# A decoder block in fp32: gate sums in raw tiles, the second norm by token tile, the SH1 sums ahead of the first weight tile, a convolution tap on ScalarE, small vectors on GpSimd's queue

## The chip, the cores and the metric

The kernel runs on one core of a Trainium2 chip. TensorE (PE) multiplies matrices, PEld is its loading of the stationary operand, VectorE (DVE) and ScalarE (ACT) do elementwise work, GpSimd (POOL) little, and SyncE (SP) issues the DMAs of the weights. The metric is the device time of one execution in microseconds (us).

## The reference

One block with 256 tokens of 2048 features, everything in fp32; each weight is used once.

```python
mod = silu(c) @ w_ada + b_ada                     # c: one vector of 2048
sh1, sc1, g1, sh2, sc2, g2 = split(mod, 6)
h = rms_norm(x, norm1_g) * (1 + sc1) + sh1
q, k, v, gb, gc, xt = split(h @ w_in, 6)          # 6 x 1024 columns
q, k = rms_norm per head (8 heads of 128)
attn = causal softmax attention(q, k, v)          # 256 tokens are one block
conv = gb * causal_dwconv(gc * xt, conv_w, conv_b)      # 3 taps
mixed = concat(rms_norm(attn), rms_norm(conv))
x = x + g1 * (mixed @ w_out)
h2 = rms_norm(x, norm2_g) * (1 + sc2) + sh2
u = causal_dwconv(h2 @ w_ffn_up, ffn_conv_w, ffn_conv_b)  # 11264 columns
ug, uu = split(u, 2)
x = x + g2 * ((silu(ug) * uu) @ w_ffn_down)
```

## The kernel before

Every weight is split in two on the chip: ScalarE rounds a tile to `hi` (`split_hi`, L246) and VectorE subtracts to get `lo` (`split_lo`, L252). Activations have such halves too, and each product is three matmuls: hi by hi, hi of the weight by lo of the activation, and lo by hi (`mm_tok`, L412 to L415).

The work is a list of slots, one weight tile of about 1 MB each: 48 for `w_in` (the table `turns` sets their order; g, c, v, x, q, k name the six parts, two banks of PSUM for each half), 16 for `w_out`, and then the up and down projections of the FFN in four segments. For slots of `w_in`, the sum of one part stays in its PSUM banks from one slot to the next if the two lie at most `near` slots apart; otherwise it is copied out by ScalarE (L424) or added by VectorE (L426) to `pa_*`. Weights arrive in a ring of raw tiles (`raw`); whoever consumes one calls `load_next`, which puts the next load on SyncE's queue. A tile is split two slots ahead (`LA`).

Beside the weights, 96 MB of `w_ada` have to be multiplied by one vector. These sums (`Ada`, SC1 and SH1 for the first norm, G1 and G2 the gates, SC2 and SH2 for the second norm) lie between the slots, tile by tile, either on TensorE (L297) or on VectorE (L303); the table `ada` says which, and from which slot on. The result is turned into columns (`cols`, L341 to L358: `adac`, `adaz`, `A`, `B`) or, for a gate, spread over the partitions (`spread`, L369).

All other work (convolution, attention, norms, evacuations) is a task with a slot number and a class from the table `cls`, which decides its place in the slot's order. Each engine works through its own list in the order in which the program issues it.

The start: x is loaded and squared, then two tiles of SC1, the first weight tile and two tiles of SH1 are loaded in that order (L1123: `steps[:2] + [("w", 0)] + steps[2:] + [("w", 1)]`). The sums of SC1 and SH1 run on TensorE between the transposes of x (`xn`), and the first `h_chunks` turns them into the first activations `h`, on ScalarE (L862, L864).

The second norm stands between `w_out` and the up-projection: the last product `m('C', 3)`, its evacuation `z` with the gate and the addition to `x1` (`evac_c`, L501, L506), the squares, the root (`n2m`, `n2q`), a diagonal matrix of the reciprocal norms (`n2d`, L604), a product of ones with it that spreads the norm over all partitions (`n2b`, L606), a copy of that (`rB`, L610) and the first `h2` (L629 to L634). TensorE has four tiles of an `ada` sum to do meanwhile. In the up-projection, a product has hi and lo of the activation side by side as 512 columns (L795), which VectorE adds up after (L688), or, where `direct` says so, each by itself with 256 columns into the same half of a bank, with no addition:

```python
for w, v in ((hi, 0), (hi, 1), (lo, 0)):
    mm(o, w[:, j, a], h2T[k + j][:, v * 256:v * 256 + 256], ...)
```

## Time and profile before

| what | value |
|---|---|
| median of 3 runs | 1180.21 us (1179.96 to 1181.82) |
| the profiled execution | 1182.36 us |
| its span | 1180.5 us |
| TensorE busy | 1153.6 us, 98% |
| VectorE busy | 934.8 us, 79% |
| ScalarE busy | 620.3 us, 53% |
| DMA queue of the weights | 314.83 MB, 74.4% of 16 engines |

The span is the time from the first to the last instruction; the 1.9 us around it belong to the execution's own time. An engine's busy time is a sum over stages, which the stretches of the span tell apart. Idle time stands in brackets ahead of the instruction that followed it, with the instruction that released it.

### The profile page before, as it was taken

How to read it: one execution, taken by the hardware profiler on the slowest of the kernel's cores; microseconds unless marked ns; L12 is line 12 of the kernel's file. 1: busy time of each engine (PE TensorE's matmuls, PEld its weight loads, DVE VectorE, ACT ScalarE, POOL GpSimd, SP SyncE). 2: the span in 40 equal slices, each digit the busy share in tenths (PEclk: the TensorE clock that was granted, in tenths of full speed). 3: DMA queues.
4: the chain of work that ended last, by engine and by line, in shares of the span. 5: the costliest groups of instructions: out<-in, count | busy, mean ns of one | idle time of the engine just before them, and what ended most of it. 6: DMA issues, size and time to landing. Idle time of an engine off the chain costs nothing.

```text
span 1180.5 us, 15371 instructions
## 1 busy us (share of the span) xinstructions
PE 1153.6 (98%) x5971; PEld 964.6 (82%) x5971; DVE 934.8 (79%) x1060; ACT 620.3 (53%) x890; POOL 1.2 (0%) x8
## 2 busy tenths in 40 slices
PE   5999999999999999999999999999999999999998
PEld 3777788878877878888888888888888888888887
DVE  3588999999999989989988766887655676576876
ACT  5645265468584555476665434555444455335442
POOL 0000000000000000000000000000000000000000
PEclk9999999999999999999999999999999999999999
DMA  9999999998878789964567988655565556766352
GB/s 364 382 348 389 384 344 376 414 366 319 319 280 308 285 297 330 384 237 155 178 222 259 372 324 319 234 195 179 194 230 172 189 179 208 234 210 203 135 169 89
DMA packets 189181, 317.98 MB, mean 269 GB/s; under 512 B 6922, under 2 KB 106028, under 8 KB 184756
## 3 DMA queue, kind: packets, MB, share of 16 engines
q1 hardware_dynamic: 187780, 314.83, 74.4%
q10 hardware_dynamic: 1328, 2.16, 0.5%
q8 instruction: 47, 0.77, 0.3%
q14 instruction: 26, 0.21, 0.0%
HBM read 312.77 MB, written 4.19 MB: 268 GB/s over the span
## 4 chain that ended last, share of the span: by engine, by line
PE 81%; DVE 10%; DMA 4%; ACT 2%; issue 1%; SPq 0%; ACTq 0%; DVEq 0%
PE z L795 23%; PE z L798 12%; DVE lo L252 4%; DVE ada L303 3%; DMA raw<-in_w_in_dram 2%; PE ada L297 1%; PE mg L414 1%; PE mg L415 1%; PE mg L412 1%; PE mx L414 1%; DMA raw<-in_w_ffn_up_dram 1%; PE mx L415 1%; PE mx L412 1%; DMA raw<-in_w_ada_dram 1%; PE mc L414 1%
## 5 line engine op out<-in xcount | busy, mean ns | idle before, releaser
L252 DVE TENSOR_TENSOR lo<-raw,hi 128x2048 fp32r<-128x2048 f32 (+2 forms) x204 | 448.2, 2204 | 141.5 <-ACT hi L246 125.4
L246 ACT ACTIVATE hi<-raw 128x2048 fp32r<-128x2048 f32 (+2 forms) x204 | 376.1, 1850 | 299.5 <-DMA raw<-in_w_in_dram 80.0
L795 PE MATMUL z<-h,hi 128*128 128x512 f32 x1408 | 329.7, 390 | 2.6 <-DVE h L634 2.0
L795 PEld LDWEIGHTS z<-h,hi 128*128 128x128 f32 x1408 | 261.1, 188 | 56.2 <-DVE h L634 1.4
L303 DVE SCALAR_TENSOR_TENSOR ada<-raw,csil,ada 128x512 f32<-128x512 f32 (+2 forms) x150 | 183.8, 1229 | 3.3 <-DMA raw<-in_w_ada_dram 0.2
L798 PEld LDWEIGHTS z<-h,lo 128*128 128x128 f32 x1408 | 174.8, 192 | 3.4
L798 PE MATMUL z<-h,lo 128*128 128x256 f32 x1408 | 176.0, 283 | 0.0
L688 DVE TENSOR_TENSOR ub<-z,ub 128x256 f32<-128x256 f32 x112 | 39.6, 417 | 34.4 <-ACT ub L685 34.3
L685 ACT ACTIVATE ub<-z 128x256 f32<-128x256 f32 x112 | 33.4, 383 | 35.3 <-PE z L795 35.3
L720 ACT ACTIVATE gh<-uy 128x512 fp32r<-128x512 f32 x22 | 13.9, 632 | 66.8 <-DVE uy L718 66.8
L702 ACT ACTIVATE uy<-ub,fc,fc 128x256 f32<-128x256 f32 x88 | 45.6, 600 | 1.9 <-DVE ub L693 1.9
L709 DVE SCALAR_TENSOR_TENSOR uy<-ub,fc,uy 128x254 f32<-128x254 f32 x88 | 42.5, 484 | 3.1
L707 DVE SCALAR_TENSOR_TENSOR uy<-ub,fc,uy 128x255 f32<-128x255 f32 x88 | 42.1, 479 | 0.1
L297 PE MATMUL ada<-raw,crep 128*32 128x256 f32 (+1 forms) x224 | 23.1, 530 | 7.6 <-DMA raw<-in_w_ada_dram 7.6
L714 ACT ACTIVATE uy<-uy 128x512 f32<-128x512 f32 x22 | 13.8, 627 | 29.7 <-DVE uy L709 29.7
L721 DVE TENSOR_TENSOR gl<-uy,gh 128x512 fp32r<-128x512 f32 x22 | 15.2, 693 | 15.4 <-ACT gh L720 15.4
L414 PE MATMUL mc<-hi,h 128*128 128x512 f32 x64 | 25.6, 400 | 1.1 <-ACT pa_x L424 1.1
L414 PE MATMUL mv<-hi,h 128*128 128x512 f32 x64 | 25.4, 397 | 0.7 <-ACT h L864 0.7
L414 PE MATMUL mg<-hi,h 128*128 128x512 f32 x64 | 25.7, 401 | 0.0
L414 PE MATMUL mx<-hi,h 128*128 128x512 f32 x64 | 25.4, 397 | 0.0
L414 PE MATMUL mk<-hi,h 128*128 128x512 f32 x64 | 25.3, 396 | 0.0
L415 PE MATMUL mq<-hi,hl 128*128 128x512 f32 x64 | 25.0, 391 | 0.2 <-DVE hl L869 0.2
(560 smaller groups left out, 1792.7 us busy)
## 6 DMA issues: line engine op xcount, KB each, us to landing
raw<-in_w_ada_dram SPq DMA_DIRECT2D x96, 1024.0 KB
raw<-in_w_ffn_up_dram SPq DMA_DIRECT2D x176, 512.0 KB
raw<-in_w_in_dram SPq DMA_DIRECT2D x48, 1024.0 KB
raw<-in_w_ffn_down_dram SPq DMA_DIRECT2D x24, 1024.0 KB
raw<-in_w_ffn_down_dram SPq DMA_DIRECT2D x24, 768.0 KB
raw<-in_w_out_dram SPq DMA_DIRECT2D x16, 1024.0 KB
xr<-in_x_dram SPq DMA_DIRECT2D x2, 1024.0 KB
x<-in_x_dram SPq DMA_DIRECT2D x8, 256.0 KB
```

Source lines behind the costliest of these rows:

```text
L246: act(hi[:, :nk], t[:, :nk], AF.Copy)
L252: V.tensor_tensor(out=lo[:, :nk], in0=t[:, :nk], in1=hi[:, :nk].bitcast(F32), op=ALU.subtract)
L297: mm(self.acc[q:q + 32, :], crep[:, i, :], t[:, j, :], start=(r == 0 and j < 4), stop=(r == self.tiles - 1 and j >= self.rows - 4), tile_p ...
L303: V.scalar_tensor_tensor(out=self.acc, in0=t[:, j, :], scalar=csil[:, i:i + 1], in1=self.acc, op0=ALU.mult, op1=ALU.add)
L414: mm(o, a, hi[:, k, s], start=(first and k == 0), stop=False)
L415: mm(o, b, hi[:, k, s], start=False, stop=False)
L688: V.tensor_tensor(out=d, in0=zp[grp][ft][:, :256], in1=d, op=ALU.add)
L702: act(y, b, AF.Identity, bias=fcols[3][:, i:i + 1], scale=fcols[2][:, i:i + 1])
L707: V.scalar_tensor_tensor(out=y[:, 1:], in0=b[:, :255], scalar=fcols[1][:, i:i + 1], in1=y[:, 1:], op0=ALU.mult, op1=ALU.add)
L709: V.scalar_tensor_tensor(out=y[:, 2:], in0=b[:, :254], scalar=fcols[0][:, i:i + 1], in1=y[:, 2:], op0=ALU.mult, op1=ALU.add)
L795: mm(zp[grp][ft], hi[:, j, ft * P:(ft + 1) * P], h2T[k + j], start=begins and j == 0, stop=ends and j == 3)
L798: mm(zp[grp][ft][:, :256], lo[:, j, ft * P:(ft + 1) * P], h2T[k + j][:, :256], start=False, stop=False)
```

## The change

The tables get new values throughout: another order of the slots of `w_in` (it begins with g and c), other slots for the tasks, `near` from 1 to 3, six raw tiles for five, fewer 2 KB buffers. Beyond that:

- `consume` begins with all four tiles of SC1 and SH1, then the first two weight tiles; the first of these is loaded in two halves. TensorE's list at the start has 30 products of constants (`idle`, `spin`). The first slot (`go_first`) takes all hi products ahead of the lo products; its `h` is made by VectorE.
- Of the second quarter of SC1 (L297 before), the sum is on VectorE.
- The sums of G1 and G2 lie in a raw tile (`home`) that is filled with zeros and the bias by GpSimd, which drops the eight loads and additions of the bias.
- The eleven small vectors (`load_v`) are loaded from GpSimd's queue, six slots earlier.
- In the short convolution, the middle tap is multiplied on ScalarE and added by VectorE for two tiles at once (`conv3`, `taps`). Two heads of the attention share a tile when they are split. The sums of squares over attention and convolution (`ss_cols`) go to TensorE one slot later than the last square.
- `evac_c` works by token tile, and the second token tile in two halves of a bank each; each token tile has its own root and its own `n2d`; the first two chunks of `h2` read `n2b` in PSUM, and `rB` is copied behind them.
- `direct` from [0, 0] to [1, 0]: 12 slots of the up-projection.

```diff
- 'bufs': [42, 6, 5, 3, 3],
+ 'bufs': [38, 6, 6, 3, 5],
+ 'spin': [22, 4, 0, 0, 4, 0],
+ 'taps': [1, 0, 0],
- 'near': 1,
+ 'near': 3,
- 'direct': [0, 0],
+ 'direct': [1, 0],
...
+        def home(self):
+            what = f"ada{self.part}_{self.c0}"
+            self.acc = sb.tile([P, 4, 512], F32, tag="raw", bufs=N_RAW, name=what).rearrange("p a b -> p (a b)")
+
+            nc.gpsimd.memset(self.acc, 0.0)
+            a = self.part * D + self.c0 * P
+            nc.gpsimd.dma_start(self.acc[0:1, :], b_ada[0:1, a:a + self.n])
...
+        one(0, slice(0, 512), 0)
+        one(1, slice(0, 256), 1)
+        root(0, 0)
+        one(1, slice(256, 512), 2)
+        nrm["p"] = bank("n2b")
+        diag(0)
+        root(1, 2)
+        diag(1)
...
-        mm(p[:, :256], ones, d, start=True, stop=True)
+        for t in range(2):
+            mm(p[:, t * P:(t + 1) * P], ones, nrm["d", t], start=True, stop=True)
...
+        ks = list(range(cut[0]))
+        h2_chunks(ks[:2], p[:, :256])
         act(rB[0], p[:, :256], AF.Copy)
-        h2_chunks(range(cut[0]), p[:, :256])
+        h2_chunks(ks[2:], rB[0])
...
+                z = t2k("tap")
+                for j in range(2):
+                    s = slice(j * 256, j * 256 + 256)
+                    act(z[:, s], b[:, s], AF.Copy, scale=w[2 - d][:, i + j:i + j + 1])
+                V.tensor_tensor(out=pair(y)[:, :, d:], in0=pair(z)[:, :, :256 - d], in1=pair(y)[:, :, d:], op=ALU.add)
...
-    consume += steps[:2] + [("w", 0)] + steps[2:] + [("w", 1)]
+    consume += steps + [("w", 0), ("w", 1)]
...
+    def spin(i):
+        for _ in range(CFG["spin"][i]):
+            mm(idle[:, :P], ones, ident, start=True, stop=True)
+
     ccol = to_cols(vc, 16, "ccol")
+    spin(0)
...
-                  (q_norm_g, 1), (k_norm_g, 1)], nc.sync)
+                  (q_norm_g, 1), (k_norm_g, 1)], nc.gpsimd)
```

TensorE's list at the start, before (`ada_0_138` is SC1, `ada_0_199` is SH1, `xn` the transposes of x):

```order
L188 MATMUL pv_ccol<-ident,vcb 128x16
L297 MATMUL ada_0_138<-raw,crep 32x256 x16
L188 MATMUL pv_vbc<-ident,vcb 128x112
L1167 MATMUL xn_163<-ident,xr 128x128 x4
L341 MATMUL adac_0_173<-ident,adae_0_170 128x128 x2
L1167 MATMUL xn_185<-ident,xr 128x128 x4
L1167 MATMUL xn_192<-ident,xr 128x128 x4
L297 MATMUL ada_0_199<-raw,crep 32x256 x8
L1167 MATMUL xn_210<-ident,xr 128x128 x4
L1167 MATMUL xn_217<-ident,xr 128x128 x4
L1167 MATMUL xn_224<-ident,xr 128x128 x4
L297 MATMUL ada_0_199<-raw,crep 32x256 x8
```

And now (`ada_0_164` is SC1, `ada_0_228` SH1, `idle` the products of constants):

```order
L194 MATMUL pv_ccol<-ident,vcb 128x16
L1204 MATMUL idle<-ident,ones 128x128 x22
L314 MATMUL ada_0_164<-raw,crep 32x256 x8
L1204 MATMUL idle<-ident,ones 128x128 x4
L314 MATMUL ada_0_164<-raw,crep 32x256 x8
L194 MATMUL pv_vbc<-ident,vcb 128x112
L1234 MATMUL xn_195<-ident,xr 128x128 x4
L349 MATMUL adac_0_203<-ident,adae_0_189 128x128 x2
L1234 MATMUL xn_209<-ident,xr 128x128 x4
L1234 MATMUL xn_214<-ident,xr 128x128 x4
L1234 MATMUL xn_219<-ident,xr 128x128 x4
L314 MATMUL ada_0_228<-raw,crep 32x256 x8
```

Ahead of the two tiles of SC1 now stand 22 and 4 products that use no data from memory; three groups of transposes for two precede SH1.

VectorE's list at the second norm, before, from the last evacuation on:

```order
L501 SCALAR_TENSOR_TENSOR z30_3661<-m('C', 3)0_3585,rC_3213,ada2_0_1535 128x512
L506 TENSOR_TENSOR x1_03_2573<-z30_3661,x1_03_2573 128x512
L501 SCALAR_TENSOR_TENSOR z31_3666<-m('C', 3)1_3586,rC_3213,ada2_0_1535 128x512
L506 TENSOR_TENSOR x1_13_2581<-z31_3666,x1_13_2581 128x512
L599 SCALAR_TENSOR_TENSOR n2m_3671<-n2q_3660,ss2_94 128x2
L200 RECIPROCAL n2r_3672<-n2q_3660 128x2
L201 SCALAR_TENSOR_TENSOR n2q_3660<-n2r_3672 128x2
L202 TENSOR_TENSOR n2q_3660<-n2q_3660,n2m_3671 128x2
L203 SCALAR_TENSOR_TENSOR n2r_3672<-n2q_3660,n2r_3672 128x2
L604 TENSOR_SCALAR n2d_3692<-ident_70,n2r_3672 128x128 x2
L629 SCALAR_TENSOR_TENSOR h2f_3699<-x1T00_3504,A2_92,n2b_3695 128x256
L629 SCALAR_TENSOR_TENSOR h2f_3703<-x1T00_3504,A2_92,n2b_3695 128x256
```

And now:

```order
L610 SCALAR_TENSOR_TENSOR z30_3668<-m('C', 3)0_3542,rC_3204,ada2_0_1428 128x512
L616 TENSOR_TENSOR x1_03_2954<-z30_3668,x1_03_2954 128x512
L610 SCALAR_TENSOR_TENSOR z31_3669<-m('C', 3)1_3543,rC_3204,ada2_0_1428 128x256
L616 TENSOR_TENSOR x1_13_2962<-z31_3669,x1_13_2962 128x256
L620 SCALAR_TENSOR_TENSOR n2m_3665<-n2q_3664,ss2_94 128x1
L610 SCALAR_TENSOR_TENSOR z31_3669<-m('C', 3)2_3544,rC_3204,ada2_0_1428 128x256
L614 SCALAR_TENSOR_TENSOR ss2_94<-n2q_3664,ss2_94 128x1
L616 TENSOR_TENSOR x1_13_2962<-z31_3669,x1_13_2962 128x256
L206 RECIPROCAL n2r_3667<-n2t_3666 128x1
L207 SCALAR_TENSOR_TENSOR n2t_3666<-n2r_3667 128x1
L208 TENSOR_TENSOR n2t_3666<-n2t_3666,n2m_3665 128x1
L209 SCALAR_TENSOR_TENSOR n2r_3667<-n2t_3666,n2r_3667 128x1
```

The second token tile (`z31`) comes in two halves, the root of the first token tile no longer waits for the second, and one reciprocal of two columns has become two of one.

TensorE's list where the up-projection begins, before (`z0_0` to `z0_3` are the four banks of the first group):

```order
L555 MATMUL x1t31_3746<-ident_70,x1_03_2573 128x128
L555 MATMUL x1t31_3746<-ident_70,x1_13_2581 128x128
L795 MATMUL z0_0_3753<-h2_0_3701,hi_3555 128x512
L795 MATMUL z0_1_3754<-h2_0_3701,hi_3555 128x512
L795 MATMUL z0_2_3755<-h2_0_3701,hi_3555 128x512
```

And now:

```order
L561 MATMUL x1t31_3779<-ident_70,x1_03_2954 128x128
L561 MATMUL x1t31_3779<-ident_70,x1_13_2962 128x128
L833 MATMUL z0_0_3786<-h2_0_3733,hi_3519 128x256 x2
L833 MATMUL z0_0_3786<-h2_0_3733,lo_3538 128x256
L833 MATMUL z0_1_3787<-h2_0_3733,hi_3519 128x256 x2
L833 MATMUL z0_1_3787<-h2_0_3733,lo_3538 128x256
```

The product with hi and lo side by side has become two of 256 columns, with the product of the weight's lo behind them.

## Rows read from the trace of the kernel before

**Rows 1.** From the page's first section (busy time of each engine, share of the span, instructions) and, from its fourth section, the chain of work that ended last, by engine.

```profile
PE 1153.6 (98%) x5971; PEld 964.6 (82%) x5971; DVE 934.8 (79%) x1060; ACT 620.3 (53%) x890; POOL 1.2 (0%) x8
...
PE 81%; DVE 10%; DMA 4%; ACT 2%; issue 1%; SPq 0%; ACTq 0%; DVEq 0%
```

**Rows 2.** From the timeline of ScalarE at the start: start, duration, engine, line, operation, output and inputs, count, and in brackets the idle time before it and what ended it. It is the second half of x that is waited for.

```profile
9.09 1.91 ACT L1150 ACTIVATE j<-xr 128x2048 f32<-128x2048 f32 x1 [0.76 <-DMA xr<-in_x_dram]
```

**Rows 3.** From the timeline of TensorE from the start to the second weight tile, with the same columns.

```profile
4.65 0.25 PE L188 MATMUL pv_ccol<-ident,vcb 16*128 16x16 f32 x1 [4.65 <-DMA vcb<-in_c_dram]
11.80 1.94 PE L297 MATMUL ada<-raw,crep 128*32 128x256 f32 x16 [6.90 <-DMA raw<-in_w_ada_dram]
14.42 1.94 PE L297 MATMUL ada<-raw,crep 128*32 128x256 f32 x16 [0.69 <-DMA raw<-in_w_ada_dram]
18.55 0.69 PE L341 MATMUL adac<-ident,adae 128*128 128x128 f32 x2 [0.96 <-ACT adae L313]
19.03 1.91 PE L1167 MATMUL xn<-ident,xr 128*128 128x128 f32 x8
20.88 1.93 PE L297 MATMUL ada<-raw,crep 128*32 128x256 f32 x16
24.49 1.07 PE L297 MATMUL ada<-raw,crep 128*32 128x256 f32 x16
28.09 0.49 PE L414 MATMUL mv<-hi,h 128*128 128x512 f32 x1 [0.72 <-ACT h L864]
...
34.04 1.93 PE L297 MATMUL ada<-raw,crep 128*32 128x256 f32 x32
```

**Rows 4.** From the timeline of ScalarE between the last sum of SH1 and the first weight product.

```profile
25.62 0.38 ACT L313 ACTIVATE adae<-ada 128x256 f32<-128x256 f32 x1 [0.33 <-PE ada L297]
27.62 0.42 ACT L864 ACTIVATE h<-hf 128x256 fp32r<-128x256 f32 x1
```

**Rows 5.** From busy time by stretch: start and end, length, then busy time and number of instructions of PE, PEld, DVE, ACT and POOL, the granted clock of TensorE, the share of the DMA engines and GB/s.

```profile
0.00:30.00 30.00, 15.59 (x109) 9.34 (x110) 9.53 (x26) 15.65 (x24) 1.22 (x8) 1.00 0.98 365
30.00:60.00 30.00, 28.91 (x173) 21.27 (x173) 17.67 (x18) 18.60 (x24) 0.00 (x0) 1.00 1.01 382
60.00:100.00 40.00, 39.78 (x191) 29.04 (x190) 30.98 (x32) 18.49 (x26) 0.00 (x0) 1.00 0.95 356
100.00:200.00 100.00, 100.00 (x461) 79.18 (x460) 96.98 (x97) 47.53 (x79) 0.00 (x0) 1.00 0.97 369
168.00:182.00 14.00, 14.00 (x63) 11.54 (x63) 12.36 (x14) 12.81 (x23) 0.00 (x0) 1.00 0.67 239
182.00:200.00 18.00, 18.00 (x81) 14.92 (x80) 17.89 (x14) 6.64 (x19) 0.00 (x0) 1.00 1.01 392
```

**Rows 6.** From what TensorE waited for: instruction, releaser, then us in total, times, longest.

```profile
PE z L795 <- DVE h L634: 2.0, 2, 1.2
PE ssA L1022 <- DVE sq L1015: 1.1, 1, 1.1
PE mc L414 <- ACT pa_x L424: 1.1, 1, 1.1
PE ssC L1022 <- DVE cv L1015: 0.7, 1, 0.7
PE z L795 <- ACT ada L348: 0.5, 1, 0.5
```

**Rows 7.** From the timeline of SyncE's queue (DMA issues) around the load of the small vectors: the first of the eleven small loads and the first load of a weight tile behind them.

```profile
167.31 0.50 SPq L162 DMA_DIRECT2D v<-in_norm_g_dram  x1
...
177.64 1.91 SPq L280 DMA_DIRECT2D raw<-in_w_ada_dram  x2
```

**Rows 8.** From the timeline of VectorE around the second norm, columns as in rows 2.

```profile
434.31 0.75 DVE L501 SCALAR_TENSOR_TENSOR z<-m('C', 3)1_3586,rC,ada 128x512 f32<-128x512 f32 x1 [1.17 <-PE m('C', 3)1_3586 L412]
439.55 0.87 DVE L629 SCALAR_TENSOR_TENSOR h2f<-x1T,A,n2b 128x256 f32<-128x256 f32 x2 [1.27 <-ACT rB L610]
```

**Rows 9.** From the timeline of TensorE around the second norm.

```profile
434.20 3.64 PE L297 MATMUL ada<-raw,crep 128*32 128x512 f32 x32
438.42 0.67 PE L606 MATMUL n2b<-n2d,ones 128*128 128x256 f32 x2 [0.58 <-DVE n2d L604]
...
441.14 2.11 PE L795 MATMUL z<-h,hi 128*128 128x512 f32 x8 [1.18 <-DVE h L634]
```

**Rows 10.** From the timeline of TensorE in one slot of the up-projection: 32 products 256 columns wide and 16 that are 512 wide.

```profile
503.31 4.00 PE L798 MATMUL z<-h,lo 128*128 128x256 f32 x32
507.14 3.82 PE L795 MATMUL z<-h,hi 128*128 128x512 f32 x16
```

**Rows 11.** From the timeline of TensorE where one whole fp32 product of 512 columns runs by itself (two records).

```profile
347.00 1.02 PE L369 MATMUL adab<-ada,ones 128*128 128x512 f32 x2
```

**Rows 12.** From the timeline of ScalarE at the first exponential of the attention.

```profile
250.43 1.28 ACT L967 ACT_TABLE_LOAD   x1 [2.99 <-DVE m L966]
```

**Rows 13.** From the timeline of ScalarE ahead of the wait of `mc` in rows 6.

```profile
51.58 1.91 ACT L246 ACTIVATE hi<-raw 128x2048 fp32r<-128x2048 f32 x1 [5.09 <-DMA raw<-in_w_in_dram]
53.40 2.04 ACT L424 ACTIVATE pa_x<-mx 128x512 f32<-128x512 f32 x4
```

More of the change, by code (lines that the diff above doesn't have):

```diff
@@ L288, in consume @@
             t = self.view(take())
[L289 removed]
+            if r == 0 and self.acc is None:
                 what = f"ada{self.part}_{self.c0}"
[L291 to L292 removed]
+                self.acc = (bank(what) if self.pe else t4k(what) if self.n > 512 else t2k(what))[:, :self.n]
             for j in range(self.rows):
@@ L459, in go, with go_first @@
                 mm_tok(f, hi[:, h::len(fs)], lo[:, h::len(fs)], [hT[k + j] for j in range(m)], m, new[h], end[h])
-        slots.append((pair_load(k, fs[0]) if len(fs) == 2 else w_load(w_in, k, 4, [(COL[fs[0]] * 512, 512)]), 4, go))
+        def go_first(hi, lo, fs=fs, end=[not near(f, 1) for f in fs]):
+            for f in fs:
+                mainp[f] = [bank(f"m{f}{t}") for t in range(2)]
+            for low in (False, True):
+                for k in range(2):
+                    for h, f in enumerate(fs):
+                        for v in hT[k][:1 if low else 2]:
+                            for t in range(2):
+                                mm(mainp[f][t], v[:, t * P:(t + 1) * P], (lo if low else hi)[:, 2 * k + h],
+                                   start=k == 0 and not low and v is hT[k][0], stop=low and k == 1 and end[0])
+        slots.append((pair_load(k, fs[0]) if len(fs) == 2 else w_load(w_in, k, 4, [(COL[fs[0]] * 512, 512)]), 4,
+                      go if i else go_first))
         for f in fs:
@@ L572, in go @@
         def go(hi, lo, part=part, f=f, k=k, tf=n == len(seq) - 1):
-            mm_tok((part, f), hi, lo, [mixT[k + j] for j in range(4)], 4, k % 8 == 0, k % 8 == 4, tf, tf and CFG["tail1"])
+            mm_tok((part, f), hi, lo, [mixT[k + j] for j in range(4)], 4, k % 8 == 0, k % 8 == 4, tf, (part, f) == ("C", 3))
             if k % 8 == 4:
@@ L1005, in att_o, with ss_cols @@
         mm(p[:, 128:256], v[1], pt[:, 256:], start=False, stop=True)
-        att[h] = (p, mix_tile(h, p[:, :256], gain["A"][:, h:h + 1]))
-    sums = {}
+        both = h // 2 in two
+        if not both:
+            two[h // 2] = t2k("my"), t2k("sq")
+        y, q = two[h // 2]
+        one = slice(h % 2 * 256, h % 2 * 256 + 256)
+        act(y[:, one], p[:, :256], AF.Copy, scale=gain["A"][:, h:h + 1])
+        act(q[:, one], p[:, :256], AF.Square)
+        if both:
+            hi, lo = t2k("mixh", F32R), t2k("mixl", F32R)
+            act(hi, y, AF.Copy)
+            V.tensor_tensor(out=lo, in0=y, in1=hi.bitcast(F32), op=ALU.subtract)
+            for j, s in enumerate((slice(0, 256), slice(256, 512))):
+                mixT[h // 2 * 2 + j] = hi[:, s], lo[:, s]
+    sums, two = {}, {}
+    def ss_cols(w):
+        p = bank("ss" + w)
+        n = sums[w].shape[1] // 256
+        for t in range(2):
+            for j in range(n):
+                a = j * 256 + t * P
+                mm(p[:, t:t + 1], sums[w][:, a:a + P], ones[:, 0:1], start=j == 0, stop=j == n - 1)
+        V.tensor_copy(ssA if w == "A" else ssC, p[:, :2])
+        done.add("ss" + w)
     def add_square(w, q, first, last):
@@ L1016, in add_square @@
         if last:
-            p = bank("ss" + w)
-            n = sums[w].shape[1] // 256
-            for t in range(2):
-                for j in range(n):
-                    a = j * 256 + t * P
-                    mm(p[:, t:t + 1], sums[w][:, a:a + P], ones[:, 0:1], start=j == 0, stop=j == n - 1)
-            V.tensor_copy(ssA if w == "A" else ssC, p[:, :2])
+            if CFG["sslag"]:
+                at(now[0] + CFG["sslag"], ss_cols, w)
+            else:
+                ss_cols(w)
     def att_q(h):
-        _, q = att.pop(h)
-        done.add(f"ss{h}")
-        add_square("A", q, len([1 for g in range(8) if f"ss{g}" in done]) == 1,
+        assert h % 2 and h in mixT and h - 1 in mixT
+        done.update((f"ss{h - 1}", f"ss{h}"))
+        add_square("A", two[h // 2][1], len([1 for g in range(8) if f"ss{g}" in done]) == 2,
                    all(f"ss{g}" in done for g in range(8)))
     def out_norm(w, s):
-        assert all(f"ss{h}" in done for h in range(8)) if w == "A" else {"cq0", "cq1"} <= done
+        assert "ss" + w in done
         r = const.tile([P, 2], F32, name="r" + w)
```

358 lines of the change are left out of this document (184 added, 174 removed), and 25 rows, old and new, of the table CFG.

## The prediction

> **What bounds the kernel now.** I read the page's busy times and its chain first: TensorE is busy 1153.6 of 1180.5 us, and the chain lies on it for 81% of the span [rows 1]. So a gain must either take work from TensorE or remove time in which it waits, and there are only 1180.5 − 1153.6 = 26.9 us of that. The stretches show where: 14.4 us of it lie before 30 us, and from 60 to 200 us there is almost none [rows 5]. The timeline of the start says what they are: TensorE multiplies SC1 at 11.80 and 14.42 and SH1 at 20.88 and 24.49, and the first weight product is at 28.09 [rows 3]. The list of waits gives the rest: single stops of 0.5 to 1.2 us, each with its releaser [rows 6]. Between 100 and 200 us VectorE too is busy 96.98 of 100 us, so there TensorE has hardly any room to come earlier than VectorE and the DMAs (0.97 busy, 369 GB/s) allow [rows 5]. A head start won at the beginning must be paid out of VectorE's idle time before 100 us. That is the question of this change.
>
> **The start.** A tile of 1 MB reaches its engine about every 2.7 us: the second half of x at 9.09 [rows 2], SC1 at 11.80 and 14.42 [rows 3]. In the new order SH1 follows, so I put it at 17.1 and 19.8, and the halves of the first weight tile at 21.1 and 22.5. In before, TensorE came to the last SH1 tile only at 24.49, because it had been at the lower speed: 16 records took 1.94 us at 11.80, 14.42 and 20.88 and 1.07 at 24.49, and ahead of the rise it had worked without a gap from 18.55 on [rows 3]. The granted clock reads 1.00 in that stretch all the same [rows 5], so of the two levels, 1.2 and 2.4 GHz, the durations tell more than that column. The 26 idle products give it such work from 4.9 on, after `pv_ccol` at 4.65 [rows 3]. What do 22 of them take? A whole fp32 product of 512 columns took 1.02 us [rows 11]; a quarter of the columns is 0.25, and at the lower speed 0.25 × 1.94/1.07 = 0.46. That is 5.6 to 10.2 us, from 4.9 to between 10.5 and 15.1. I take some of each, an end near 12, so SC1 is late by nothing that matters. Then the last SH1 tile runs from 19.8 to 20.9. From its end to the first weight product before passed 28.09 − 25.56 = 2.5 us, through `adae` at 25.62 and the last `h` on ScalarE [rows 3, 4]. With the same chain the first product comes at 23.4; 0.1 for the second half of the weights. That is **−4.6 us**, with −5.3 (chain shortened by VectorE's `h`) and +3.6 (below, as a rival) as ends.
>
> The Trainium skill has this as a rule (TensorE: Matmul & The Clock Gate, What's actually happening): the engine stands throttled by default, and activity releases it to twice the speed. By that rule the 22 products end early and SC1 takes 1.07 from the first; the records' 1.94 against 1.07 agree with it, the clock column does not show it.
>
> **SC1 moved.** Two 1 MB tiles leave TensorE; two such took 1.93 us at 34.04 [rows 3]. **−1.9 us.** VectorE gets 16 instructions of 256 columns; two of about that kind took 0.87 [rows 8], so 16 × 0.44 = 7.0 us. From 30 to 100 us VectorE is busy 17.67 + 30.98 of 70 us [rows 5], so it has 21.4 us of room for them; the cover holds unless it is already needed for the head start, see the rivals.
>
> **The stop at `mc`.** 1.1 us [rows 6]: `pa_x` on ScalarE begins at 53.40, behind a `hi` that waited 5.09 us for a DMA [rows 13]. In the new order of slots other banks are evacuated there. I take it as gone, **−1.1**; ends 0 and −1.1.
>
> **Does the head start last?** −4.6 − 1.9 − 1.1 = −7.6 at about 57 us. For it VectorE must do 7.6 us more work before 100 us, and 7.0 for SC1: 14.6 of the 21.4 it has. Where near = 3 saves additions of `pa` it gets some back. The DMAs: the eleven small vectors stand on SyncE's queue from 167.31 to 177.64 [rows 7], and the rate from 168 to 182 us is 239 GB/s against 392 behind it [rows 5]; (392 − 239)/392 × 14 = 5.5 us of supply lost. On GpSimd's queue they no longer stop the weights. So supply moves forward by about as much as TensorE does. I take 0.6 as given back, **+0.6** (ends 0 and +5).
>
> **Sums of squares.** `ss_cols` one slot later: `ssA` and `ssC` waited 1.1 and 0.7 us [rows 6]. A slot is some 6 us, so what was late is done. **−1.8.** What could be late next is the norm that hangs on them, which moves by two slots for one of the two. Ends 0 and −1.8.
>
> **The second norm.** Before: `n2b` at 438.42, 0.58 us after the four `ada` tiles that TensorE had to do from 434.20 to 437.84 [rows 9]. The halves and the token tiles shorten VectorE's path (z at 434.31 [rows 8]): it works on half the width behind the last product. The fill then ends last, so I can win no more than the 0.58; I take 0.5. Then `h2f` at 439.55 waits for `rB` on ScalarE [rows 8]; `n2b` ends at 439.09, so reading it at once is worth 0.46. Together about **−1.0**; ends 0 and −1.3. The second `h2` chunk pair now waits for `rB`, but TensorE has 24 products for the first two.
>
> **The up-projection.** 12 slots with 16 wide products become 384 of 256 columns instead of 192 of 512. The pitch is (3.82 − 0.39)/15 = 0.229 and (4.00 − 0.28)/31 = 0.120 [rows 10], if the last record's length is taken off. 192 × (0.240 − 0.229) = **+2.1**; ends 0 and +4. VectorE loses 24 additions, which it does not need: nothing waits there for it. The last products of `w_out` and of the down-projection are halved for one token tile: 42 products at 0.011 us = **+0.5**. In the same region two stops of 0.8 (`h` of L634, 2.0 less 1.18 at 441.14 [rows 6, 9]) and 0.5 (`ada` of L348) may go; the order of the tasks around them is new, I take half: **−0.6**; ends 0 and −1.3.
>
> **ScalarE and the rest.** ScalarE gets two more table loads in the attention, of 1.28 us [rows 12], eight tap copies and the small copies. It is busy 53% of the span [rows 1], so I cost it at 0, with ends −1 and +2.6: two loads, if the exponentials that wait behind each hold a product up. The Trainium skill (ScalarE: Activation LUTs, What ACT_TABLE_LOAD costs) adds a drain to each load, 2.66 us in all; by that the upper end would be 5.3. The row shows the 1.28 alone. The gate sums' eight fewer loads and additions lie on VectorE, which has them beside TensorE's work: 0. The tail after the last product is the same work: 0.
>
> **The sum.** −4.6 − 1.9 − 1.1 + 0.6 − 1.8 − 1.0 + 2.1 + 0.5 − 0.6 = −7.8. The profiled execution has 1182.36 and would have 1174.6; the median is 2.15 below it, so 1180.2 − 7.8 = **1172.4 us**.
>
> **Rivals.** *(a) Supply eats the head start.* VectorE is full from 100 us on [rows 5]. If its 7.0 us for SC1 leave too little room, all but 2.5 us of the 7.6 is lost by 200 us: sum −7.8 + 4.5 = −3.3, 1176.9 us. For it speaks 96.98%; against it the 21.4 us of idle time before and the hole in the loads that closes.
>
> *(b) The idle products come in the way.* They are ahead of SC1 on TensorE's queue. If all run at the lower speed, SC1 begins at 15.1 instead of 11.80, 3.3 later; if everything behind it stays at that speed as before, the first weight product comes at up to 31.7. More likely the rise comes midway, and it comes at 26: −2.1 for −4.6, 1174.9; the worst is 1180.6. For it speaks that 22 × 0.46 passes 11.80; against it that unbroken work ended the lower speed before.
>
> *(c) Banks held longer.* With near = 3, sums stay in PSUM over up to three slots, and six raw tiles change nothing in the eight banks. If a first product of a slot must then wait for ScalarE's four copies (2.04 us [rows 13]) as `mc` did, it costs 1.1 us each time. From seven such stops on, the gain is gone; at twelve, +13.2 − 7.8 = +5.4, 1185.6 us: slower. For it speaks the stop that exists; against it that near = 1 held banks as well and had only that one.
>
> **How the numbers follow.** This kernel's measurement can tell 0.2%, 2.4 us. The forecast has 0.62, with 1168 to 1176 as its own range (start −5.3, no halved loss, or supply by 3 worse); (a) 0.18, of which two thirds are below 1177.8; (b) 0.11; (c) 0.09. Faster: 0.62 + 0.12 + 0.08 = 0.82 less 0.02 for a forecast that misses upward, 0.80; same 0.11; slower 0.09. The range has to hold eight in ten: from 1165.5, where every end is taken at its best but two, to 1179.5, which takes in (a) and most of (b).
>
> **What would show it.** The first weight product near 23.5 and SC1 at about 11.8 to 12.5 with 1.07 for 16 records (else (b)). The slots from 100 to 300 us some 7 us earlier than before, without new stops of TensorE (else (a): waits for `lo` or `hi` from VectorE; (c): waits for ScalarE's `pa` copies). No hole in the weights' rate near 170 us. `ssA` and `ssC` without a wait. `n2b` right behind the four `ada` tiles. Wide products of 12 slots with a pitch of 0.120. The forecast is wrong if the first product is later than 26 or if TensorE's waits between 60 and 430 us exceed those of before by over 4 us.

## The result and the profile after

The changed kernel takes 1170.93 us in the median (1170.62 to 1170.94, four runs), the one before 1180.09 in the same series (1179.02 to 1181.82). The ratio is 0.992, with a 95% interval of 0.9903 to 0.9938: 9.2 us less, where 7.8 were forecast. The traced executions stand further apart: the span fell from 1180.5 to 1169.1, by 11.4 us, because the traced execution of before lay 2.2 us above its own median and that of after does not. What made that execution of before longer than the others can't be told from its one trace; e7, whose list of work at the start is the same as in before, points at the start, where its first weight product came 2.7 us earlier.

The page of the changed kernel, the busy times and the chain by engine:

```profile
PE 1156.2 (99%) x6239; PEld 983.9 (84%) x6239; DVE 915.7 (78%) x1025; ACT 628.5 (54%) x909; POOL 12.0 (1%) x23
...
PE 96%; DMA 2%; ACT 1%; SPq 1%; DVE 1%; issue 0%; ACTq 0%; DVEq 0%
```

Against [rows 1], TensorE has 2.6 us more work and yet the span is shorter: its idle time went from 26.9 to 1169.1 − 1156.2 = 12.9 us. VectorE, 10% of the chain before, is down to 1%. So time did not come from work taken off TensorE, but from stops that went.

Busy time by stretch, with the columns of [rows 5]:

```profile
0.00:30.00 30.00, 23.34 (x186) 18.98 (x186) 11.16 (x28) 19.38 (x27) 4.75 (x15) 1.00 0.98 365
30.00:60.00 30.00, 29.07 (x153) 21.27 (x152) 24.84 (x35) 18.52 (x29) 0.00 (x0) 1.00 1.05 408
...
168.00:182.00 14.00, 14.00 (x63) 11.60 (x62) 12.05 (x11) 9.46 (x14) 2.81 (x2) 1.00 0.52 190
```

Of the 14.0 us that TensorE won, 23.34 − 15.59 = 7.8 lie in the first 30 us, but part of that is the products of constants. VectorE now does 24.84 of 30 us between 30 and 60 instead of 17.67, so it works off more, earlier. One row speaks against the prediction: from 168 to 182 us the weights come at 190 GB/s, a deeper hole than the one before (239), though the small vectors are gone from that queue. The longest wait of SyncE's queue between 164 and 177 us (us in total, times, longest) and GpSimd's timeline in that stretch say where it comes from:

```profile
SPq L290 <- DVE ada L320: 11.6, 1, 11.6
...
174.29 2.30 POOL L298 MEMSET ada<- 128x2048 f32 x1 [78.89 <-DVE lo L262]
```

Loads are issued at 164.18 and then not before 176.19, because VectorE, which frees the raw tiles, finishes with only one between 164.2 and 176.1 us: the `lo` that ends at 174.18. In between it takes `pa_c` and four `hl`, each of which waits for ScalarE. The one free tile goes to the gate's sum (one call of `load_next` issues no load), which makes up 2.0 of the 12.0 us; the rest is VectorE's order of work. No stop of TensorE follows from the hole in this kernel, as its list of waits shows (us in total, times, longest; the ones left out belong to the start):

```profile
...
PE z L833 <- ACT h L672: 0.2, 1, 0.2
...
PE mv L422 <- ACT pa_c L432: 0.2, 1, 0.2
```

Every wait of [rows 6] is gone but the first `z`, which is down from 1.18 to 0.24. The order of the milestones in the two traces: the first weight product came 3.5 us earlier (28.09 to 24.57), the product `mv` that begins the 36th weight tile 5.8 (239.13 to 233.37), the first product of the up-projection 11.9 (441.14 to 429.21), the last product 11.5 (1175.62 to 1164.17). So about a half of the gain was there by 240 us, the other half came between 240 and 440, and the FFN neither gave nor took much. From the 36th weight tile to the first product of the up-projection, before and after:

```profile
239.13:441.14 202.01, 196.95 (x969) 159.24 (x967) 189.12 (x238) 129.61 (x259) 0.00 (x0) 1.00 0.85 309
233.37:429.21 195.84, 195.60 (x999) 161.31 (x998) 184.59 (x226) 131.19 (x251) 0.00 (x0) 1.00 0.89 317
```

Of the 6.2 us between these two, 4.8 are idle time of TensorE that went (5.06 to 0.24), and 1.4 are less busy time for the same weight tiles.

The timeline of TensorE at the start:

```profile
4.14 7.01 PE L1204 MATMUL idle<-ident,ones 128*128 128x128 f32 x44
11.44 1.07 PE L314 MATMUL ada<-raw,crep 128*32 128x256 f32 x16 [0.29 <-DMA raw<-in_w_ada_dram]
...
17.32 1.07 PE L314 MATMUL ada<-raw,crep 128*32 128x256 f32 x16
...
20.83 1.07 PE L314 MATMUL ada<-raw,crep 128*32 128x256 f32 x16 [0.52 <-DMA raw<-in_w_ada_dram]
...
24.57 3.93 PE L484 MATMUL mg<-hi,h 128*128 128x512 f32 x16 [1.42 <-ACT h L1267]
```

The 22 products end at 11.15, the records of `ada` take 1.07 from the first tile on, and SH1's second tile ends at 21.9. The second norm, on TensorE:

```profile
423.79 3.64 PE L314 MATMUL ada<-raw,crep 128*32 128x512 f32 x32
427.36 0.73 PE L645 MATMUL n2b<-n2d,ones 128*128 128x128 f32 x4
...
429.21 0.91 PE L833 MATMUL z<-h,hi 128*128 128x256 f32 x2 [0.24 <-ACT h L672]
```

`n2b` follows the four `ada` tiles without a stop, and `h2f` on VectorE follows it without the copy:

```profile
428.13 0.87 DVE L670 SCALAR_TENSOR_TENSOR h2f<-x1T,A,n2b 128x256 f32<-128x256 f32 x2 [0.58 <-PE n2b L645]
```

### The profile page after: what moved, and what is told of

Same layout as the page of the kernel before. It is cut to its first block, busy times and chain, and to the rows that moved or that the text cites. A ratio compares the mean times of both kernels' runs of the same rounds, so it can differ in the third digit from the quotient of the medians.

```text
span 1169.1 us, 15911 instructions
## 1 busy us (share of the span) xinstructions
PE 1156.2 (99%) x6239; PEld 983.9 (84%) x6239; DVE 915.7 (78%) x1025; ACT 628.5 (54%) x909; POOL 12.0 (1%) x23
## 4 chain that ended last, share of the span: by engine, by line
PE 96%; DMA 2%; ACT 1%; SPq 1%; DVE 1%; issue 0%; ACTq 0%; DVEq 0%
PE z L847 24%; PE z L850 12%; PE z L833 6%; PE mx L422 1%; PE mq L422 1%; PE mk L422 1%; PE mx L423 1%; PE mq L423 1%; PE mk L423 1%; PE mx L420 1%; PE mq L420 1%; PE mk L420 1%; PE mv L422 1%; PE mv L420 1%; PE ada L314 1%; PE mv L423 1%
## 5 line engine op out<-in xcount | busy, mean ns | idle before, releaser
L847 PE MATMUL z<-h,hi 128*128 128x512 f32 x1216 | 283.8, 390 | 0.0
L847 PEld LDWEIGHTS z<-h,hi 128*128 128x128 f32 x1216 | 225.8, 188 | 45.3
L320 DVE SCALAR_TENSOR_TENSOR ada<-raw,csil,ada 128x512 f32<-128x512 f32 (+3 forms) x167 | 195.3, 1175 | 5.5 <-DMA raw<-in_w_ada_dram 2.0
L850 PEld LDWEIGHTS z<-h,lo 128*128 128x128 f32 x1216 | 151.0, 192 | 3.0
L850 PE MATMUL z<-h,lo 128*128 128x256 f32 x1216 | 152.0, 283 | 0.0
L718 DVE SCALAR_TENSOR_TENSOR uy<-ub,fc,uy 128x254 f32<-128x254 f32 (+1 forms) x176 | 71.4, 477 | 0.2
L833 PE MATMUL z<-h,hi 128*128 128x256 f32 x384 | 69.9, 284 | 0.4 <-ACT h L672 0.2
L750 DVE TENSOR_TENSOR ub<-z,ub 128x256 f32<-128x256 f32 x88 | 31.1, 416 | 41.6 <-ACT ub L747 41.6
L833 PEld LDWEIGHTS z<-h,hi 128*128 128x128 f32 x384 | 59.9, 192 | 0.8 <-ACT h L672 0.5
L833 PE MATMUL z<-h,lo 128*128 128x256 f32 x192 | 54.3, 283 | 0.0
L747 ACT ACTIVATE ub<-z 128x256 f32<-128x256 f32 x88 | 26.3, 384 | 27.6 <-PE z L847 27.6
L833 PEld LDWEIGHTS z<-h,lo 128*128 128x128 f32 x192 | 36.8, 192 | 0.0
L422 PE MATMUL mq<-hi,h 128*128 128x512 f32 x64 | 25.4, 397 | 0.0
```

What stands on the lines that cost most here:

```text
L320: V.scalar_tensor_tensor(out=self.acc, in0=t[:, j, :], scalar=csil[:, i:i + 1], in1=self.acc, op0=ALU.mult, op1=ALU.add)
L422: mm(o, a, hi[:, k, s], start=(first and k == 0), stop=False)
L718: V.scalar_tensor_tensor(out=o[:, d:], in0=v[:, :256 - d], scalar=w[2 - d][:, i + j:i + j + 1], in1=o[:, d:], op0=ALU.mult, op1=ALU.add)
L750: V.tensor_tensor(out=d, in0=zp[grp][ft][:, :256], in1=d, op=ALU.add)
L833: mm(o, w[:, j, a], h2T[k + j][:, v * 256:v * 256 + 256], start=begins and j == 0 and w is hi and not v, stop=ends and j == 3 and w is lo)
L847: mm(zp[grp][ft], hi[:, j, ft * P:(ft + 1) * P], h2T[k + j], start=begins and j == 0, stop=ends and j == 3)
```

## The experiments

All are the changed kernel with one edit, but for e7, which is the kernel before with one edit. Times are medians; "before" in their series was 1180.2 to 1180.5.

**e1: no products of constants.**

```diff
- 'spin': [22, 4, 0, 0, 4, 0],
+ 'spin': [0, 0, 0, 0, 0, 0],
```

> The changed kernel without its 30 products of constants at the start. Theory (TensorE bounds the kernel, and what it loses at the start stays lost): the tiles of SC1 and the first of SH1 take 1.9 us for 16 records instead of 1.07, the last SH1 tile begins near 24 instead of 20.83, the first weight product comes at 27.5 to 28 instead of 24.57, and the time is 1170.9 + 3 = about 1174. Rival (VectorE and the DMAs are full from 100 us on, so a later start is made up there): first product as late, but slot 20 as in the changed kernel and a time within 0.7 of 1170.9.

Measured: 1170.92 (1170.71 to 1171.1), so nothing. But the rival's reason is not right either: the first product was hardly late, 24.99 for 24.57. TensorE's timeline:

```profile
11.46 1.94 PE L314 MATMUL ada<-raw,crep 128*32 128x256 f32 x16 [7.19 <-DMA raw<-in_w_ada_dram]
...
19.23 1.07 PE L314 MATMUL ada<-raw,crep 128*32 128x256 f32 x16
...
21.26 1.07 PE L314 MATMUL ada<-raw,crep 128*32 128x256 f32 x16
...
24.99 3.92 PE L484 MATMUL mg<-hi,h 128*128 128x512 f32 x16 [1.42 <-ACT h L1267]
...
30.89 1.07 PE L314 MATMUL ada<-raw,crep 128*32 128x256 f32 x16 [0.17 <-DMA raw<-in_w_ada_dram]
```

The tiles of SC1 took 1.94 us, as before the change, and the rise of the speed came between them and 19.23, with no products of constants. SH1's second tile ran at 21.26 without a wait; in the changed kernel it ran at 20.83, after waiting 0.52 us for its DMA. What was left, 0.4 us at the first product, vanished in a wait that comes right behind: the tile at 31 us waits for its DMA in either kernel and begins 0.1 us earlier here. So that load sets the start, and 30 products change nothing.

**e2: the old order of the loads at the start.**

```diff
-    consume += steps + [("w", 0), ("w", 1)]
+    consume += steps[:2] + [("w", 0)] + steps[2:] + [("w", 1)]
...
     ada_init[0].consume(1)
+    w = take()
```

> The changed kernel with the loads at the start in the old order: SC1, SC1, first weight tile, SH1, SH1, second weight tile; the products of constants stay. Theory: each SH1 tile comes one tile later (2.7 us), the first weight product at 26.5 to 27.3 instead of 24.57, the time about 1173.3. Rival (supply makes it up): a time within 0.7 of 1170.9.

Measured: 1174.43 (1171.99 to 1174.69), 3.5 us more. The first product came at 28.88, 4.3 us later, of which 2.8 were still there from slot 6 to slot 36. The order of loads is worth most of the head start, and what is still lost at slot 6 is not made up behind it. One of the four executions, at 1171.99, lost only 1.1 us; why is not known. Here the granted clock shows a drop, with TensorE idle 3.2 us at once for the moved SH1 tile:

```profile
0.00:30.00 30.00, 20.16 (x167) 16.14 (x168) 7.03 (x24) 15.18 (x24) 4.76 (x15) 0.94 0.98 364
```

**e3: the second quarter of SC1 back on TensorE.**

```diff
-         [4, 12, 512, False, 67, 6], [1, 8, 1024, False, 8, 12], [1, 2, 256, False, 1, 2],
+         [4, 12, 512, False, 67, 6], [1, 8, 1024, False, 8, 12], [1, 2, 256, True, 1, 2],
```

> The changed kernel with the second quarter of the SC1 sum back on TensorE (two tiles of 1.07 us), which takes 16 instructions, some 7 us, from VectorE before 60 us. Theory: TensorE is what counts and VectorE had room: +2.1 us, 1173.0. Rival (VectorE's head start is what counts): the freed VectorE time lets later slots come earlier, 1170 to 1171.

Measured: 1172.13 (1172.07 to 1172.23), 1.2 us more. Two tiles of 1.07 are 2.1; by the slots' starts the first tile cost 1.1, the second 0.5, and what remained at slot 6 was 1.0, partly because the wait of 0.2 us for `pa_c` in the same stretch goes away when TensorE is later. TensorE's work counts, and VectorE had room for the 16 instructions.

**e4: five raw tiles.**

```diff
- 'bufs': [38, 6, 6, 3, 5],
+ 'bufs': [38, 6, 5, 3, 5],
```

> The changed kernel with five raw tiles instead of six, so four while a gate's sum holds one (the rate of the weights between 168 and 182 us fell to 190 GB/s in the changed kernel although the small vectors were gone from that queue, and GpSimd clears the raw tile for the gate at 174.29). Theory: the loads had slack of some tiles, so new stops of TensorE between 160 and 240 us of 2 us at most, 1171 to 1173. Rival (the ring is what sets the supply): stops in many slots, over 1176.

Measured: 1186.41 (1183.55 to 1188.94), 15.5 us more, and slower than before. What TensorE waited for:

```profile
PE ada L314 <- DMA raw<-in_w_ada_dram: 4.5, 5, 2.8
PE ssC L1066 <- DVE cv L1075: 3.3, 1, 3.3
PE ap L1030 <- ACT s L1022: 2.4, 1, 2.4
PE m('C', 1)0_3126 L422 <- ACT ada L378: 1.2, 1, 1.2
```

Four stops of 1.2 to 3.3 us (the first line has other, short waits too). They add up to 9.7 us, and the first product of the up-projection is 15.0 us late; the granted clock has the rest. Behind the first of them, a stop of 2.80 us ahead of 156.72:

```profile
157.00:160.00 3.00, 3.00 (x14) 1.80 (x7) 2.89 (x5) 1.21 (x2) 0.00 (x0) 0.65 1.05 403
160.00:163.00 3.00, 3.00 (x12) 2.41 (x11) 3.00 (x4) 1.29 (x1) 0.00 (x0) 0.78 0.97 345
```

From 157.7 to 161.2 us the products of 512 columns begin 0.43 us apart, not 0.23. The stop cost 2.8 us and the products behind it 1.1 more. Behind the stops of 2.4 and 3.3 us the clock is 0.57 from 253 to 257 and from 376 to 380 us, behind the one of 1.2 it stays at 1.00. At these shares three times 1.7 us of work are lost, and 9.7 + 5.1 = 14.8 of the 15.0. The stops are few, not in many slots as the rival had it, but its time holds, and I had taken the slack for larger. The first stop comes before a gate's sum takes a tile (GpSimd clears it at 178.98 in this trace), so five tiles are too few there even without one. That the three later stops come from the ring was not followed back.

**e5: no 256-column products in place of the wide ones.**

```diff
- 'direct': [1, 0],
+ 'direct': [0, 0],
```

> The changed kernel with direct [0, 0]: the 384 products of 256 columns are 192 of 512 again, and VectorE adds the halves in 24 instructions. Theory (TensorE alone counts there, 0.011 us for each of 192): 1170.9 - 2.1 = 1168.8. Rival (VectorE's additions delay the h2 of the second half, and the stops of 0.7 and 0.95 us near 500 and 512 us return): 1170.0 to 1171.5, with those stops in the trace.

Measured: 1172.86 (1172.65 to 1173.42), 1.9 us more. Of TensorE's waits, those of the up-projection:

```profile
PE z L847 <- DVE h L675: 2.0, 2, 1.2
PE adac L349 <- DVE ub L750: 0.9, 1, 0.9
PE z L847 <- ACT ada L356: 0.5, 1, 0.5
PE z L847 <- DVE ub L750: 0.3, 1, 0.3
```

The theory falls: 3.7 us of waits for 0.2, against less work on TensorE. Busy time from the first product of the up-projection to the last of all, here and in the changed kernel:

```profile
429.75:1166.06 736.31, 733.37 (x3915) 634.89 (x3916) 540.93 (x611) 368.35 (x435) 2.31 (x2) 1.00 0.66 225
429.21:1164.17 734.96, 734.83 (x4108) 645.48 (x4108) 533.84 (x588) 369.78 (x436) 2.31 (x2) 1.00 0.67 225
```

TensorE saves 1.5 us (734.83 to 733.37), where 2.1 were reckoned. Of the waits, 2.9 us have to do with VectorE's 24 additions: two end with an addition (0.3 and 0.9), and near 490 and 502 us the columns of an `ada` sum and the steps of `h2` come later in VectorE's list (1.86 us for the `h2f` at 500.30). The 0.85 us ahead of the first product are another matter: no addition has run by then, but a product of 512 columns needs hi and lo of `h2` and so waits for VectorE's `h`, where the first of 256 needs only hi, from ScalarE. The rival had the mechanism, with too small a size.

**e9 and e10: 256-column products in three of the six groups.**

```diff
-                if seg == 0 and n < len(cut) + 1 and CFG["direct"][min(n, 1)]:
+                if seg == 0 and n < len(cut) + 1 and CFG["direct"][min(n, 1)] and grp < 3:
```

(e10: `grp >= 3`.)

> The changed kernel with the 256-column products only in the first three of the six groups (6 slots instead of 12): 12 of VectorE's 24 additions come back, half of the 2.0 us more TensorE work goes. In the run without any of them the stops of TensorE came back: 0.4 to 1.0 us at the first product, 0.44 after it, 1.05, 0.70 and 1.31 from 482 to 502 us. Theory (the stops near 482 to 502 belong to the additions of the last groups): these stops return, about 3 us, and 1170.9 - 1.0 + 3 = 1173. Rival (half of the additions are room enough): no stop over 0.4 us after 440, 1169.9.

> The changed kernel with the 256-column products only in the last three of the six groups. Theory (the additions of the last groups are those that delay VectorE at 482 to 502 us): the stops at the first product return (1.0 us for 0.8, and 0.44), those from 482 on do not, 1170.9 - 1.0 + 0.6 = 1170.5. Rival (VectorE's work of the first groups is still queued then): stops from 482 on of 2 to 3 us, 1172.5.

Measured: 1171.49 (1171.35 to 1171.92) with the first three, 1170.70 (1170.62 to 1171.62) with the last three. With the first three, two stops came back (0.5 and 0.8 us, near 489 and 501), not the one near 482: 1.3 us where the theory had 3, and more than the rival's none. With the last three the waits of that stretch are

```profile
PE z L847 <- DVE h L675: 0.9, 1, 0.9
...
PE z L847 <- DVE ub L750: 0.3, 1, 0.3
```

that is, only those at its beginning (ahead of 429.7 and 442.5), as expected. That makes it the best of the versions tried, by 0.2 us against the changed kernel, which the measurement can't tell from none.

**e6: the old places of the attention's steps.**

```diff
- 'heads': [2, 7, 8, 4, 5, 5, 4, 4],
- 'head_steps': [1, 1, 2, 3, 5],
+ 'heads': [4, 4, 7, 2, 4, 5, 5, 4],
+ 'head_steps': [1, 1, 2, 3, 4],
...
- 'qk': [[3, 5], [3, 7]],
+ 'qk': [[4, 5], [0, 7]],
```

> The changed kernel with the old places of the attention's steps (the tables heads, head_steps and qk), so also without the two extra table loads of 1.28 us. Theory (the stops of before between 245 and 268 us, 2.6 us, went because six raw tiles let ScalarE's hi come earlier, not because of the places): within 0.8 of 1170.9. Rival 1 (the places removed them): stops of 1 to 2.6 us in that stretch, 1172 to 1173.5. Rival 2 (the table loads cost): 1168.4 to 1169.5.

Measured: 1173.92 (1173.63 to 1174.18), 3.0 us more. New waits:

```profile
PE trc L1124 <- DVE pa_c L1118: 1.2, 2, 1.0
PE ap L1030 <- ACT s L1022: 0.9, 1, 0.9
```

Up to slot 36 the two kernels run alike (this one 0.3 us ahead). At slot 39 it is 2.7 us later, but part of that is work that it does earlier. At slot 46 it is 1.1 us late (309.08 for 307.96); 1.6 more come at the stop of `trc`, a transpose of the convolution, ahead of 323.61, so that it begins `w_out` at 326.39 for 323.65 and stays 2.8 late:

```profile
309.08 0.48 PE L422 MATMUL mg<-hi,h 128*128 128x512 f32 x1
...
326.39 0.47 PE L422 MATMUL m('A', 0)0_2819<-hi,mixh 128*128 128x512 f32 x1
```

So rival 1 holds for about a half: the places are worth 3.0 us in the changed kernel, 1.4 of it up to slot 46, with one stop of 0.9 in the attention; the rest is a stop that the kernel before does not have. The stops of before in that stretch are 0.8 and 0.3 us, not the 2.6 of the theory. The two table loads are gone here and no gain shows; since the places changed with them, the run does not price them.

**e7: the kernel before with six raw tiles.**

```diff
- 'bufs': [42, 6, 5, 3, 3],
+ 'bufs': [38, 6, 6, 3, 3],
```

> The kernel before with six raw tiles instead of five (and 38 small tiles of 2 KB instead of 42, to make room), nothing else. Theory (the ring is what made ScalarE's hi late in before: it waited 80.0 us for w_in's DMAs there and 41.7 in the changed kernel): the stops from 245 to 268 us go, that wait falls to some 40 us, and the time is 2 to 3.5 us under before, about 1177.5. Rival (the order of the tasks made them): within 0.7 of before.

Measured: 1188.56 (1188.23 to 1188.87), 8.1 us more than before. ScalarE's `hi` waited 44.3 us for the DMAs of `w_in` instead of 80.0, and at slot 6 to 30 this kernel was 1.95 us ahead. That head start is from the start, where TensorE's list is the same as in before, but SH1 takes 1.07 from its first tile and the first product comes 2.7 us earlier than in the trace of before (28.09):

```profile
19.22 1.07 PE L297 MATMUL ada<-raw,crep 128*32 128x256 f32 x16
...
25.38 0.50 PE L414 MATMUL mv<-hi,h 128*128 128x512 f32 x1 [0.72 <-ACT h L864]
```

Whether the sixth tile or the execution made that difference was not tried. Of the waits of TensorE

```profile
PE m('D', 1, 0)0_7008 L414 <- ACT gh L720: 3.5, 1, 3.5
PE mk L414 <- DVE v1c L190: 1.4, 1, 1.4
PE as L957 <- ACT kT L950: 0.7, 1, 0.7
PE ap L983 <- ACT s L975: 0.5, 1, 0.5
```

`as` and `ap` stand where they stood: my theory falls, and that agrees with e6. The head start was lost again, mostly at 222.79 in the wait for `v1c` (1.4), and the wait of 3.5 us for `gh` that ends at 845 was followed by the lower clock (0.50 from 846 to 850), 6.9 us together. I made room for the sixth tile by taking four small ones, and which of the two edits makes `gh` late was not tried apart. The run shows that six raw tiles at the price of four small ones are worth nothing to the kernel before.

**e8: the sums of squares at once.**

```diff
- 'sslag': 1,
+ 'sslag': 0,
```

> The changed kernel with the sums of squares on TensorE right after the last square, as before. Theory: the stops of ssA and ssC return, 1.1 to 1.5 and 0.7 us, so 1172.7 to 1173.2. Rival (with the earlier supply the last squares are ready anyway): within 0.5 of 1170.9.

Measured: 1184.92 (1183.38 to 1185.35), 14.0 us more, from one number in a table. The waits:

```profile
PE ssC L1066 <- DVE cv L1075: 4.3, 1, 4.3
...
PE ssA L1066 <- DVE sq L1075: 3.4, 1, 3.4
```

The stops were not the 1.1 and 0.7 of before, since in the new order the last squares come later against TensorE's list: 3.4 and 4.3 us. And 14 − 7.7 = 6.3 us came after them. By stretch, from the end of the stop for `ssA` on:

```profile
346.60:349.00 2.40, 2.36 (x10) 2.29 (x11) 0.48 (x2) 0.00 (x0) 0.00 (x0) 0.50 1.04 395
...
351.00:353.00 2.00, 2.00 (x7) 1.52 (x6) 1.97 (x3) 0.00 (x0) 0.00 (x0) 0.56 1.02 413
```

From 353 to 355 us the clock reads 1.00 again. Behind the stop for `ssC` it is 0.55 from 366 to 370 us and 0.54 from there to 373.5. Of these 6.3 us the theory had nothing.

**e11: the copy of the spread norm first.**

```diff
+        act(rB[0], p[:, :256], AF.Copy)
         h2_chunks(ks[:2], p[:, :256])
-        act(rB[0], p[:, :256], AF.Copy)
```

> The changed kernel with the copy rB of the spread norm ahead of the first two chunks of h2 again. Theory: the first h2 on ScalarE waits for the copy, 0.36 to 0.46 us, and the first product of the up-projection begins so much later: 1171.3. Rival (the weights or h2's second chunk set the start of that slot): within 0.15 of 1170.9.

Measured: 1171.19 (1171.08 to 1171.69), 0.26 us more; in the trace the wait ahead of the first product is 0.66 for 0.24:

```profile
429.39 0.90 PE L833 MATMUL z<-h,hi 128*128 128x256 f32 x2 [0.66 <-ACT h L672]
```

0.42 us, as the copy takes. The theory holds.

**e12: the small vectors on SyncE's queue.**

```diff
-                  (q_norm_g, 1), (k_norm_g, 1)], nc.gpsimd)
+                  (q_norm_g, 1), (k_norm_g, 1)], nc.sync)
...
-            rows(vecs[-1], [(by_p(src), 88)], nc.gpsimd)
+            rows(vecs[-1], [(by_p(src), 88)], nc.sync)
```

> The changed kernel with the eleven small vectors on SyncE's queue again, at the same slot as now (15). Theory (they delay the weights: 10 us on that queue in before, and one raw tile less cost 15 us in the changed kernel): stops of TensorE of 2 us and more between 120 and 200 us, 1173 to 1177. Rival (six tiles cover such a hole): no new stop over 0.4 us, within 0.5 of 1170.9.

Measured: 1175.22 (1174.84 to 1175.47), 4.3 us more. SyncE's queue, the first of the small loads and the first weight behind them:

```profile
119.82 1.00 SPq L168 DMA_DIRECT2D v<-in_norm_g_dram  x1
...
130.66 1.46 SPq L290 DMA_DIRECT2D raw<-in_w_ada_dram  x3
```

And by stretch:

```profile
122.00:135.00 13.00, 13.00 (x59) 10.70 (x57) 11.70 (x11) 3.83 (x2) 0.00 (x0) 1.00 0.74 267
...
150.00:170.00 20.00, 17.51 (x78) 13.36 (x78) 17.18 (x24) 13.21 (x33) 0.00 (x0) 0.91 1.05 410
```

The rate falls to 267 GB/s, and some 20 and 27 us after the last small load TensorE stops for 0.9 us (`mq`, until 149.71) and for 2.5 (an `ada` tile, until 157.49), then runs at the lower clock for a while (0.51 from 159 to 161 us). At slot 22 this kernel is 4.7 us late and stays so. The theory holds. In the changed kernel nothing stands ahead of these loads on GpSimd's queue: seven of the eleven are issued between 1.83 and 5.4 us, the rest at 93. So the edit moves them in time too, and the run does not tell the queue from the time.

## Why the prediction was right, and where not

Forecast 1172.4 and measured 1170.93, inside the range; the sum was −7.8 and came to −9.2. The mechanism was right: stops of TensorE went, at the start, in the sums of squares and in the second norm. Its terms are less good than the sum, and that they add up so well is in part luck: the start and SC1 brought some 2 us less than forecast, the second norm, the up-projection and the stretch of the attention more.

*The start, −4.6.* The traces have −3.5, from 28.09 to 24.57. The reason given, the order of loads, is right: e2 puts it back and loses 3.5 us in the end. But the 28.09 is of one execution: the same list has its first product at 25.38 in e7, so that part of the −3.5, and of the 2.2 us by which the traced execution of before was long, may be its own. The tiles of SH1 ran at 17.32 and 20.83 where I put 17.1 and 19.8: the step of 2.7 us a tile held for the first, not for the second, which waited for its DMA and ran 3.5 us behind it. From the end of SH1 to the first product took 2.7, near the 2.5 of before. The part on the products of constants was wrong: they do what I said of the speed (1.07 from the first tile), and it is worth nothing, because without them the first product is only 0.4 us later and the load that is waited for at 31 us takes that up (e1). With that, rival (b) had no object.

*SC1 moved, −1.9.* By e3 1.0 to 1.2: the term was sized by the tiles' time, and short waits in the same stretch took the place of part of it.

*The stop at `mc`, and what is given back.* The stop is gone. By the 36th weight tile the head start was 5.8 us, for the 7.0 that the first four terms make together. Rival (a), a head start eaten by supply, did not come: whatever a run lost or won by 60 us (e2, e3) it still had at 230. VectorE had the room that I counted. The argument on the queue of the small vectors came out too, though not in the place where I put it: I wrote that the hole near 170 us would close. It did not, since VectorE frees one raw tile in 12 us there and the gate's sum takes that one. But e12 shows what the small loads on SyncE's queue would cost, 4.3 us, and e4 how little the ring has to spare.

*Sums of squares, −1.8.* Right in kind: `ssA` and `ssC` wait no more. The price of not doing it is 14.0 us in the new order of tasks (e8), so this term can't be read from the waits of before, which stood for another order.

*The second norm, −1.0.* The wait ahead of `n2b` is gone as I said, and reading it without the copy is worth 0.42 (e11) where I had 0.46. The first product came 5.4 us after the start of the `ada` tiles behind `m('C', 3)` (423.79 to 429.21) for 6.9 before (434.20 to 441.14), so −1.5: 0.6 at `n2b`, 0.4 by the copy, and 0.6 that I had not seen, because the first product of 256 columns waits only for hi of `h2` (0.24 where the wide one waits 0.85, e5 and e10).

*The up-projection, +2.1 + 0.5 − 0.6.* This term had a wait wrong. I wrote that VectorE loses 24 additions "which it does not need: nothing waits there for it", and gave the two stops near 500 and 512 us a half of a chance by themselves. They went whole (0.5 and 0.8), and by e5 and e9 additions delay what those stops wait for: with all of them TensorE waits 2.9 us behind the first product, without 0.1. TensorE pays 1.5 us for the narrow products, not 2.1. From the first product of the up-projection to the last of all, after is 0.5 us longer than before, where the terms had made it 1.7; and undoing the edit in the changed kernel costs 1.9 us, where I had forecast that it would gain.

*ScalarE and the attention, 0.* The largest miss. The stops of the attention had 0.8 and 0.3 us in the list of waits of before, and I gave the new places of its steps no term, only ends of −1 and +2.6 for table loads. Of the 6.2 us that were won between 240 and 440 us, 1.1 are these stops, 1.8 the sums of squares and 1.5 the second norm; some 1.4 are less busy time of TensorE for the same weight tiles, which no run here traces to an edit. The 3.0 us of e6 are no measure of this term, since half of them are a stop that before did not have.

*Rival (c), banks held longer,* did not come: `mv` waits 0.2 us for a `pa` copy, once. That near = 3 has no price was not tried by itself. Nor were the order of the slots, the gate sums in raw tiles, the tap on ScalarE, the second norm by token tile and the halves of the first weight tile undone alone; what each of them brings is open.

The terms taken one by one out of the changed kernel (3.5, 1.2, 1.9, 3.0, 14.0, 0.3, 4.3, 15.5 for the ring) add up to 43.7 us, for a change that brought 9.2. They are no shares of it: each edit undone alone leaves the others fitted to a time that no longer comes.

## What to carry to other kernels

Where one engine is busy for 98%, look for the engine behind each of its stops, however short the stop and however low that engine's share of the whole: 24 additions on a VectorE that idles 22% of the span cost TensorE 2.9 us of waits, more than the 1.5 us that it pays for being rid of them. A long stop is paid twice, by its length and by the lower clock behind it (e4, e8). An edit that takes a buffer out of a shared ring is paid for in the ring's depth, and how much a ring has to spare differs from stretch to stretch: with five tiles TensorE stopped at 154 us (e4), and with six of which a gate's sum held one it did not at 174. And a product that waits in TensorE's list for a sum on another engine is cheap to issue one slot later and dear to issue one slot too early.
